# Interleaving the high and low halves of the activations, so that a stationary block is read with a stride of 8 bytes

## The chip, the cores and the metric

The kernel runs on one core of a Trainium2 chip. The metric is the device time of one execution in microseconds; the median of the runs shown counts. Five engines work side by side in a core: TensorE (PE; its weight loads have a row of their own, PEld), VectorE (DVE), ScalarE (ACT), GpSimd (POOL) and SyncE (SP), which issues most of the DMAs here.

## The reference

A decoder trunk of two layers on 256 tokens of width 2048, in float32. Layer 0 mixes tokens by retention (8 heads), layer 1 by sliding-window attention (32 heads of 64, 4 key/value heads, window 128). After the mixer each layer has a SwiGLU block of width 5632 and a gated per-layer embedding; one norm ends it. Cut to what matters:

```python
for i in range(DEPTH):
    h = rmsnorm(x, norm_mix[i])
    x = x + (retention_mixer(h, ...) if i % 2 == 0 else swa_mixer(h, ...))
    x = x + swiglu(rmsnorm(x, norm_ffn[i]), ffn_w_in[i], ffn_w_out[i])
    gate = jax.nn.sigmoid(rmsnorm(x, norm_ple[i]) @ ple_w_gate[i])
    x = x + gate * (p[i] @ ple_w_proj[i])
return rmsnorm(x, norm_final)
```

Nearly all of its arithmetic is matmuls of 256 tokens with large weight matrices: two matrices in every mixer, two in every SwiGLU block, two in every embedding step.

## The kernel before, in words

**Products in three parts.** A float32 product is made of three matmuls in TensorE's faster 32-bit type (float32r). Each operand is split into `hi`, the value rounded to that type, and `lo`, what is left over; the product is `x_hi * w_hi + x_hi * w_lo + x_lo * w_hi`. `split` (lines 209 to 217) makes both halves: ScalarE writes `hi` (line 211, or 214 with a scale), then VectorE computes `lo` from the source and `hi` (line 212, or 215).

**What is stationary and what moves.** The activations, turned so that features lie on the partitions, are the stationary operand: a block is 128 features by 128 tokens, so 128 float32 in each partition. The weights move: 512 columns, which is 2048 bytes in each partition. `multiply` (line 143) issues for each unit of 256 rows of a weight matrix two blocks of features, two blocks of tokens and the three products of lines 161, 162 and 163: twelve matmuls, each with a weight load of its own.

```python
xh, xl = u.lhs.hi[:, k, sl], u.lhs.lo[:, k, sl]
nc.tensor.matmul(ch.acc[n], xh, hi[:, j, cols], start=first, stop=False)
nc.tensor.matmul(ch.acc[n], xh, lo[:, j, cols], start=False, stop=False)
nc.tensor.matmul(ch.acc[n], xl, hi[:, j, cols], start=False, stop=last)
```

**The stationary tiles.** `Lhs` (line 44) holds a pair of tiles of one layout, [128 partitions, blocks of features, 256 tokens]. There are five pairs: `xTh`/`xTl` (line 107; 16 blocks; the normed input of every input projection, gate and up matrix), `pTh`/`pTl` (line 108; 2 blocks; the per-layer embedding), `yTh`/`yTl` (line 308; 32 blocks; retention's output), `oTh`/`oTl` (line 409; 16 blocks; attention's output) and `hTh`/`hTl` (line 579; 44 blocks; the SwiGLU block's hidden layer). The first two lie in a pool that lasts, the others in a pool of their stage, opened when the stage's first unit is due. Every stationary tile of these, and every tile of the moving weights, begins at an address that leaves 160 when divided by 256 bytes; a pad of 56 floats ahead of the stage pools (line 106) is part of what makes it so.

**The order of the work.** `run` goes through the units of all stages in one sequence. For each it issues the DMA of the unit five places ahead, splits the weights of the unit three places ahead, issues the matmuls, and then lets every waiting generator in `side` take one step. Those generators do what follows a finished block of results: 32x32 transposes on VectorE (line 236), then splits into the stationary tiles (`place`, line 277, and lines 388, 552, 586, 619). TensorE meets a few other matmuls on the way: retention's scores (lines 329, 331) and outputs (356 to 358, whose stationary tiles are pairs of their own that `Lhs` does not hold), attention's scores (460), its probability transposes (512) and its outputs (544). In the last stage the final gate block is cut into pieces of 512, 256 and 256 columns.

Of the kernel before, what the change touches and what calls it, by code (L numbers as in the profile page):

```python
# [11 lines left out]
F32 = mybir.dt.float32  # L12
F32R = mybir.dt.float32r
# [5 lines left out]
P = 128  # L19
D = 2048  # L20
S = 256
# [3 lines left out]
KD = D // P  # L25
# [3 lines left out]
RET_OUT_K = RH * RV // P  # L29
# [3 lines left out]
FF_K = FF // P  # L33
PLE = 256
PLE_K = PLE // P
# [8 lines left out]
class Lhs:  # L44


    def __init__(self, tiles=None):
        self.tiles = tiles
        self.ready = set()

    hi = property(lambda self: self.tiles[0])
    lo = property(lambda self: self.tiles[1])


class Chunk:
# [32 lines left out]
def tile_trunk(ctx, tc, ins, out):  # L88
    nc = tc.nc
    pool = ctx.enter_context(tc.tile_pool(name="persist", bufs=1))  # L90
# [13 lines left out]
    turned = ctx.enter_context(tc.tile_pool(name="turned", bufs=1))  # L104

    turned.tile([P, 56], F32, name="pad")
    xT = [pool.tile([P, KD, S], F32R, name=n) for n in ("xTh", "xTl")]
    pT = [pool.tile([P, PLE_K, S], F32R, name=n) for n in ("pTh", "pTl")]


    side = deque()
# [97 lines left out]
    def split(hi, lo, src, scale=None):  # L209
        if scale is None:  # L210
            nc.scalar.activation(hi, src, AF.Copy)  # L211
            nc.vector.tensor_tensor(lo, src, hi.bitcast(F32), op=ALU.subtract)  # L212
        else:
            nc.scalar.activation(hi, src, AF.Copy, scale=scale)  # L214
            nc.vector.scalar_tensor_tensor(  # L215
                out=lo, in0=src, scalar=scale, in1=hi.bitcast(F32), op0=ALU.mult, op1=ALU.subtract
            )
# [9 lines left out]
    def transposes(dst, src):  # L227

        n = P // SQ
        src = src.rearrange("p t (k c f) -> p t k c f", c=n, f=SQ)  # L230
        dst = dst.rearrange("p k (t c f) -> p t k c f", c=n, f=SQ)
        for i in range(n * n):
            if i % STEP == 0:
                yield
            a, b = divmod(i, n)
            nc.vector.transpose(  # L236
                dst[b * SQ : (b + 1) * SQ, :, :, a, :], src[a * SQ : (a + 1) * SQ, :, :, b, :]
            )
# [5 lines left out]
    class Norm:  # L244
# [3 lines left out]
        def __init__(self, which, layer):  # L248
            self.gain = None if which is None else gains[:, which, layer, :]
            self.ss = self.inv = None  # L250
            self.lhs = Lhs(xT)
            self.seen = 0
# [28 lines left out]
    def residual(stage, norm, c, late=0):  # L281

        def done(acc):
            for t in range(NT):
                xc = xs[:, t, c * NW : (c + 1) * NW]
                nc.vector.tensor_tensor(xc, xc, acc[t], op=ALU.add)  # L288
            norm.chunk(c)

            def later():
                for _ in range(late):
                    yield
                xt = turned.tile([P, 4, S], F32, name="xt")
                yield from transposes(xt, xs[:, :, c * NW : (c + 1) * NW])
                yield from norm.places(c, xt)

            return later()

        return done  # L300


    def retention(norm, next_norm, w_in, w_out):
        yl = Lhs()

        def opened(st, pools):
            st.pool = pools.enter_context(tc.tile_pool(name="ret", bufs=2, reuse_waits="tile"))
            yl.tiles = [st.pool.tile([P, RET_OUT_K, S], F32R, name=n, bufs=1) for n in ("yTh", "yTl")]

        stage = Stage(opened)  # L310

        def head(h):
# [90 lines left out]
    def swa(norm, next_norm, w_in, w_out):  # L403
        ol = Lhs()
        st = {}

        def opened(stage, pools):
            sp = stage.pool = pools.enter_context(tc.tile_pool(name="swa", bufs=1, reuse_waits="tile"))
            ol.tiles = [sp.tile([P, KD, S], F32R, name=n) for n in ("oTh", "oTl")]
            st["rel"] = rel = sp.tile([P, 3 * P], F32, name="rel")  # L410
            nc.sync.dma_start(rel, ins["rel"])
            st["sink"] = sink = sp.tile([P, SH], F32, name="sink")
            nc.sync.dma_start(sink, ins["sinks"].to_broadcast([P, SH]))

        stage = Stage(opened)

        def kv_done(acc):
# [145 lines left out]
        n = KD // KU  # L563
# [10 lines left out]
    def ffn(layer, norm, next_norm):  # L574
        hl = Lhs()

        def opened(stage, pools):
            fp = stage.pool = pools.enter_context(tc.tile_pool(name="ffn", bufs=1, reuse_waits="tile"))
            hl.tiles = [fp.tile([P, FF_K, S], F32R, name=n) for n in ("hTh", "hTl")]
            pt = turned.tile([P, 4, S], F32, name="xt")[:, 0:PLE_K, :]  # L580
            nc.sync.dma_start(pt, ins["pT"][layer])

            def later():
                for _ in range(3):
                    yield
                split(*pT, pt)

            side.append(later())

        stage = Stage(opened)  # L590

        def pair(j):
            st = []

            def gate_done(acc):
                h = stage.pool.tile([P, NT, NW], F32, name="h")
                for t in range(NT):
                    nc.scalar.activation(h[:, t, :], acc[t], AF.Silu, scale=norm.inv[:, t : t + 1])
                st.append(h)

            def up_done(acc):
                h = st[0]
                for t in range(NT):
                    nc.vector.scalar_tensor_tensor(
                        out=h[:, t, :],
                        in0=acc[t],
                        scalar=norm.inv[:, t : t + 1],
                        in1=h[:, t, :],
                        op0=ALU.mult,
                        op1=ALU.mult,  # L610
                    )

                def later():
                    hT = turned.tile([P, 4, S], F32, name="xt")
                    yield from transposes(hT, h)
                    for i in range(0, 4, 2):
                        yield
                        ks = slice(4 * j + i, 4 * j + i + 2)
                        split(hl.hi[:, ks, :], hl.lo[:, ks, :], hT[:, i : i + 2, :])
                        hl.ready.update(range(ks.start, ks.stop))  # L620

                return later()

            stage.linear(ins["ffn_w_in"][layer], j, norm.lhs, gate_done)
            stage.linear(ins["ffn_w_in"][layer], FF // NW + j, norm.lhs, up_done)

        for j in range(FF // NW):
            pair(j)
        for c in range(4):
            stage.linear(ins["ffn_w_out"][layer], c, hl, residual(stage, next_norm, c))  # L630
        return stage
# [235 lines left out]
```

## Time and profile before

| | |
|---|---|
| median of the runs | 2625.12 us (2624.99 to 2625.26) |
| the profiled execution, its own time | 2625.55 us |
| its span, first to last instruction | 2623.4 us |
| granted TensorE clock, mean | 0.998 of full |
| weight loads and matmuls | 11643 each |
| DMA | 497.79 MB, mean 190 GB/s |

How to read it: the profile lists one execution. A line of a group names the source line, the engine, the operation, what it writes and reads, the size, the count, the busy time and the mean time of one; behind the second bar stands the idle time of the engine ahead of these instructions, and what ended it. Matmuls are pipelined and their ends are modelled, so the duration of one is longer than the step from one start to the next. A weight load (PEld) runs while the matmul ahead of it streams.

### The profile page before, as it was taken

How to read it: one execution, taken by the hardware profiler on the slowest of the kernel's cores; microseconds unless marked ns; L12 is line 12 of the kernel's file. 1: busy time of each engine (PE TensorE's matmuls, PEld its weight loads, DVE VectorE, ACT ScalarE, POOL GpSimd, SP SyncE). 2: the span in 40 equal slices, each digit the busy share in tenths (PEclk: the TensorE clock that was granted, in tenths of full speed). 3: DMA queues.
4: the chain of work that ended last, by engine and by line, in shares of the span. 5: the costliest groups of instructions: out<-in, count | busy, mean ns of one | idle time of the engine just before them, and what ended most of it. 6: DMA issues, size and time to landing. Idle time of an engine off the chain costs nothing.

```text
span 2623.4 us, 31295 instructions
## 1 busy us (share of the span) xinstructions
PE 2609.3 (99%) x11643; PEld 2145.1 (82%) x11643; DVE 1814.6 (69%) x2563; ACT 1223.1 (47%) x1531; POOL 15.1 (1%) x31
## 2 busy tenths in 40 slices
PE   9999999999999999999999999999999999999998
PEld 7888888888888888888888887777888888888887
DVE  7777777766676767676555886887757575755565
ACT  6444444444444444444444555555444444444444
POOL 0000000000000000000000000000000000000000
PEclk9999999999999999999999999999999999999999
DMA  8555555566666666666666665446666666666664
GB/s 288 187 187 187 186 186 180 182 192 186 203 191 195 191 196 189 199 187 200 193 193 194 191 196 163 126 145 188 189 198 191 197 191 198 189 197 194 193 209 144
DMA packets 139481, 497.79 MB, mean 190 GB/s; under 512 B 15808, under 2 KB 16960, under 8 KB 139200
## 3 DMA queue, kind: packets, MB, share of 16 engines
q1 hardware_dynamic: 139040, 495.73, 60.1%
q8 instruction: 91, 1.49, 0.3%
q14 instruction: 62, 0.51, 0.1%
q10 hardware_dynamic: 288, 0.07, 0.0%
HBM read 493.63 MB, written 2.10 MB: 189 GB/s over the span
## 4 chain that ended last, share of the span: by engine, by line
PE 95%; DVE 3%; issue 1%; DMA 1%; ACT 0%; ACTq 0%; POOLq 0%; POOL 0%; SPq 0%; DVEq 0%
PE acc L163 31%; PE acc L161 31%; PE acc L162 31%; DVE xt L236 1%; DVE lo L212 1%; PE at L460 1%; PE tr L512 0%; PE at L544 0%; DMA raw<-in_ret_w_in 0%; PE at L329 0%; DVE xTl L215 0%; PE at L358 0%; PE at L356 0%; PE at L357 0%; DVE xs L288 0%
## 5 line engine op out<-in xcount | busy, mean ns | idle before, releaser
L212 DVE TENSOR_TENSOR lo<-raw,hi 128x1024 fp32r<-128x1024 f32 (+1 forms) x929 | 1131.4, 1221 | 700.5 <-ACT hi L211 693.1
L211 ACT ACTIVATE hi<-raw 128x1024 fp32r<-128x1024 f32 (+1 forms) x929 | 980.7, 1058 | 1185.9 <-PE acc L163 1075.2
L161 PE MATMUL acc<-hi,xTh 128*128 128x512 f32 x2592 | 1010.8, 390 | 1.8 <-ACT xTh L214 1.7
L162 PE MATMUL acc<-lo,xTh 128*128 128x512 f32 x2592 | 1009.1, 389 | 1.4 <-DVE lo L212 1.4
L163 PE MATMUL acc<-hi,xTl 128*128 128x512 f32 x2592 | 1009.0, 389 | 0.7 <-DVE xTl L215 0.7
L161 PEld LDWEIGHTS acc<-hi,xTh 128*128 128x128 f32 x2592 | 487.4, 188 | 105.5 <-issue 2.9
L162 PEld LDWEIGHTS acc<-lo,xTh 128*128 128x128 f32 x2592 | 487.3, 188 | 103.7 <-DVE lo L212 3.1
L163 PEld LDWEIGHTS acc<-hi,xTl 128*128 128x128 f32 x2592 | 487.2, 188 | 102.4 <-DVE xTl L215 1.5
L161 PE MATMUL acc<-hi,hTh 128*128 128x512 f32 x704 | 274.1, 389 | 0.0
L162 PE MATMUL acc<-lo,hTh 128*128 128x512 f32 x704 | 274.1, 389 | 0.0
L163 PE MATMUL acc<-hi,hTl 128*128 128x512 f32 x704 | 274.1, 389 | 0.0
L236 DVE STREAM_TRANSPOSE xt<-h 32x256 f32<-32x256 f32 x352 | 153.4, 436 | 6.8
L163 PEld LDWEIGHTS acc<-hi,hTl 128*128 128x128 f32 x704 | 132.2, 188 | 27.5
L162 PEld LDWEIGHTS acc<-lo,hTh 128*128 128x128 f32 x704 | 132.2, 188 | 27.3
L161 PEld LDWEIGHTS acc<-hi,hTh 128*128 128x128 f32 x704 | 132.2, 188 | 27.3
L236 DVE STREAM_TRANSPOSE xt<-xs 32x256 f32<-32x256 f32 x320 | 139.5, 436 | 6.0
L162 PE MATMUL acc<-lo,yTh 128*128 128x512 f32 x256 | 99.7, 389 | 0.0
L161 PE MATMUL acc<-hi,yTh 128*128 128x512 f32 x256 | 99.7, 389 | 0.0
L163 PE MATMUL acc<-hi,yTl 128*128 128x512 f32 x256 | 99.7, 389 | 0.0
L214 ACT ACTIVATE xTh<-xt,gains 128x256 fp32r<-128x256 f32 x80 | 35.7, 499 | 64.5 <-DVE xt L236 60.0
L236 DVE STREAM_TRANSPOSE xt<-qk 32x256 f32<-32x256 f32 x128 | 55.8, 436 | 9.8 <-ACT qk L321 7.8
L236 DVE STREAM_TRANSPOSE xt<-y 32x256 f32<-32x256 f32 x128 | 55.9, 436 | 2.5
(128 smaller groups left out, 1170.8 us busy)
## 6 DMA issues: line engine op xcount, KB each, us to landing
raw<-in_ffn_w_in SPq DMA_DIRECT2D x352, 512.0 KB, 4.2
raw<-in_ret_w_in SPq DMA_DIRECT2D x191, 512.0 KB, 3.6
raw<-in_ffn_w_out SPq DMA_DIRECT2D x176, 512.0 KB, 4.0
raw<-in_ret_w_out SPq DMA_DIRECT2D x64, 512.0 KB, 3.7
raw<-in_ple_w_gate SPq DMA_DIRECT2D x64, 512.0 KB, 4.2
raw<-in_swa_w_in SPq DMA_DIRECT2D x40, 512.0 KB, 3.7
raw<-in_swa_w_out SPq DMA_DIRECT2D x32, 512.0 KB, 3.6
raw<-in_ple_w_proj SPq DMA_DIRECT2D x8, 512.0 KB, 3.8
```

The source lines that it names most:

```text
L161: nc.tensor.matmul(ch.acc[n], xh, hi[:, j, cols], start=first, stop=False)
L162: nc.tensor.matmul(ch.acc[n], xh, lo[:, j, cols], start=False, stop=False)
L163: nc.tensor.matmul(ch.acc[n], xl, hi[:, j, cols], start=False, stop=last)
L211: nc.scalar.activation(hi, src, AF.Copy)
L212: nc.vector.tensor_tensor(lo, src, hi.bitcast(F32), op=ALU.subtract)
L214: nc.scalar.activation(hi, src, AF.Copy, scale=scale)
L236: nc.vector.transpose(dst[b * SQ : (b + 1) * SQ, :, :, a, :], src[a * SQ : (a + 1) * SQ, :, :, b, :])
L460: nc.tensor.matmul(ats[e][:, 0:P] if b == 0 else ats[e][:, P : 3 * P], qT[sl, i, b * P : (b + 1) * P], kT[sl, j, 0 : (b + 1) * P], start=True,
```

## The change

Each pair of tiles becomes one tile with a last axis of 2: element `[..., 0]` is `hi`, `[..., 1]` is `lo`. The views `hi` and `lo` thus have a stride of 8 bytes along the tokens, for ScalarE and VectorE that write them and for TensorE that loads a block of them. A block of 128 tokens spans 1024 bytes. The moving weights keep their layout, and so do the stationary tiles of lines 356 to 358. Three pads are added ahead of the stages' tiles: 16 floats (64 bytes) for `yT`, 48 floats (192 bytes) for `oT`, 32 floats (128 bytes) for `hT`; `xT` and `pT` begin where `xTh` and `pTh` began. The four kinds of tiles so begin 0, 64, 128 and 192 bytes, modulo 256, behind the place of the moving weights.

```diff
 class Lhs:
-    def __init__(self, tiles=None):
-        self.tiles = tiles
+    def __init__(self, tile=None):
         self.ready = set()
-
-    hi = property(lambda self: self.tiles[0])
-    lo = property(lambda self: self.tiles[1])
+        if tile is not None:
+            self.take(tile)
+
+    @staticmethod
+    def shape(blocks):
+        return [P, blocks, S, 2]
+
+    def take(self, tile):
+        self.hi, self.lo = tile[:, :, :, 0], tile[:, :, :, 1]
...
-    xT = [pool.tile([P, KD, S], F32R, name=n) for n in ("xTh", "xTl")]
-    pT = [pool.tile([P, PLE_K, S], F32R, name=n) for n in ("pTh", "pTl")]
+    xT = pool.tile(Lhs.shape(KD), F32R, name="xT")
+    pT = pool.tile(Lhs.shape(PLE_K), F32R, name="pT")
...
-            yl.tiles = [st.pool.tile([P, RET_OUT_K, S], F32R, name=n, bufs=1) for n in ("yTh", "yTl")]
+            st.pool.tile([P, 16], F32, name="pad", bufs=1)
+            yl.take(st.pool.tile(Lhs.shape(RET_OUT_K), F32R, name="yT", bufs=1))
...
-            ol.tiles = [sp.tile([P, KD, S], F32R, name=n) for n in ("oTh", "oTl")]
+            sp.tile([P, 48], F32, name="pad")
+            ol.take(sp.tile(Lhs.shape(KD), F32R, name="oT"))
...
-            hl.tiles = [fp.tile([P, FF_K, S], F32R, name=n) for n in ("hTh", "hTl")]
+            fp.tile([P, 32], F32, name="pad")
+            hl.take(fp.tile(Lhs.shape(FF_K), F32R, name="hT"))
...
-                split(*pT, pt)
+                q = Lhs(pT)
+                split(q.hi, q.lo, pt)
```

## The prediction, made before the result was known

> **What bounds the kernel now.** I read the page first: the span, the engines' busy time, and the chain that ended last.
>
> ```profile
> span 2623.4 us, 31295 instructions
> ...
> PE 2609.3 (99%) x11643; PEld 2145.1 (82%) x11643; DVE 1814.6 (69%) x2563; ACT 1223.1 (47%) x1531; POOL 15.1 (1%) x31
> ...
> PE 95%; DVE 3%; issue 1%; DMA 1%; ACT 0%; ACTq 0%; POOLq 0%; POOL 0%; SPq 0%; DVEq 0%
> ```
>
> TensorE is never free: 2609.3 of 2623.4 us, and 95% of the chain. So the time is the number of matmuls times the step from one matmul to the next, and every other engine matters only where it makes PE wait. Second, the groups of matmuls by form, for their numbers (columns: count, then busy us and mean ns of one; the ns include a matmul's run-out, which overlaps the next, so they are not the step).
>
> ```profile
> L161 PE MATMUL acc<-hi,xTh 128*128 128x512 f32 x2576 | 1006.3, 391 | 1.8 <-ACT xTh L214 1.7
> L161 PE MATMUL acc<-hi,hTh 128*128 128x512 f32 x704 | 274.1, 389 | 0.0
> L161 PE MATMUL acc<-hi,yTh 128*128 128x512 f32 x256 | 99.7, 389 | 0.0
> L161 PE MATMUL acc<-hi,oTh 128*128 128x512 f32 x128 | 50.7, 397 | 0.0
> L161 PE MATMUL acc<-hi,pTh 128*128 128x512 f32 x32 | 12.5, 389 | 0.0
> L161 PE MATMUL at<-hi,xTh 128*128 128x256 f32 x16 | 4.5, 283 | 0.0
> L161 PE MATMUL acc<-hi,xTh 128*128 128x256 f32 x16 | 4.5, 280 | 0.0
> ```
>
> Lines 162 and 163 issue one matmul for each of line 161, so the matmuls whose stationary operand the change touches are 3 x (2576 + 704 + 256 + 128 + 32 + 16 + 16) = 3 x 3728 = **11184 of 11643**: xT 7824, hT 2112, yT 768, oT 384, pT 96.
>
> Third, the step, from a window of nothing but such matmuls (columns: window, its length, then busy us and count of PE, of PEld, and on).
>
> ```profile
> 900.00:1300.00 400.00, 400.00 (x1767) 331.32 (x1766) 264.17 (x330) 175.75 (x185) 0.00 (x0) 1.00 0.62 194
> ```
>
> 400 us / 1767 = **226.4 ns**, at granted clock 1.00. 11184 x 226.4 ns = 2532 us, 97% of the span: one ns on the step is 11.2 us, 0.43%. About 2% (52 us) is what a measurement of this kernel can tell from no change; that is a step 4.7 ns longer or shorter.
>
> Fourth, is the step as short as it can be? The last stage has runs of matmuls with 256 columns (six of them, then three with 512):
>
> ```profile
> 2594.05 0.28 PE L161 MATMUL acc<-hi,xTh 128*128 128x256 f32 x1
> ...
> 2594.76 0.40 PE L161 MATMUL acc<-hi,xTh 128*128 128x512 f32 x1
> ...
> 2595.46 0.28 PE L161 MATMUL acc<-hi,xTh 128*128 128x256 f32 x1
> ```
>
> Six steps in 0.71 us: 118.3 ns with 256 columns. From 256 to the usual 512 columns the step grows by 226.4 - 118.3 = 108 ns, so streaming 512 columns takes 2 x 108 = 216 ns (an estimate from these rows), and **10.5 ns of a step are something else**: 11184 x 10.5 ns = 117 us, 4.5% of the time. The change can win no more than about that through the matmuls.
>
> Fifth, what the 10.5 ns hang on. After an interruption by other matmuls the same three instructions step otherwise:
>
> ```profile
> 47.30 0.40 PE L163 MATMUL acc<-hi,xTl 128*128 128x512 f32 x1
> 47.53 0.40 PE L161 MATMUL acc<-hi,xTh 128*128 128x512 f32 x1
> 47.77 0.40 PE L162 MATMUL acc<-lo,xTh 128*128 128x512 f32 x1
> 48.00 0.39 PE L163 MATMUL acc<-hi,xTl 128*128 128x512 f32 x1
> ...
> 50.06 0.39 PE L163 MATMUL acc<-hi,xTl 128*128 128x512 f32 x1
> ```
>
> 47.30 to 48.00 is three steps of 233 ns; 47.30 to 50.06 is twelve of 230 ns; then the step settles at 226.4. Operands and shapes are the same, only the timing of the weight load against the running matmul differs. So at least part of the extra is not a fixed price: something in the load and the running stream gets in each other's way. That is what a different stride of the load can touch, in either direction.
>
> **The change part by part.** *It removes and adds no instruction*: each `hi`/`lo` pair of tiles becomes one tile with the same bytes, and three pads of 64, 192 and 128 bytes move the tiles behind them. DMAs, semaphores' causes and the order of issue stay; no step is moved past a queue.
>
> *The weight loads.* 11184 loads now read 128 elements 8 bytes apart, over 1024 bytes of a partition instead of 512. The rows of loads:
>
> ```profile
> L161 PEld LDWEIGHTS acc<-hi,hTh 128*128 128x128 f32 x704 | 132.2, 188 | 27.3
> L163 PEld LDWEIGHTS acc<-hi,yTl 128*128 128x128 f32 x256 | 48.1, 188 | 10.0
> L544 PEld LDWEIGHTS at<-pT,vs 128*64 128x64 f32 x48 | 3.7, 136 | 5.5 <-issue 4.5 <-DVE lo L212 0.7 <-DVE sc L470 0.4
> ```
>
> Busy plus idle per load is (132.2 + 27.3) / 704 = 226.6 ns, the step again. 64 columns fewer take 188 - 136 = 52 ns less, so 128 columns are read in 104 ns, the rest is latency. Even read at half speed (208 ns) the load fits under the step, and a load that is late by its latency alone costs nothing, since the 256-column run steps at 118 ns with loads that last 188. The cover is the matmul itself; past 216 ns of reading it would be gone, and each further ns would cost 11.2 us. No row of this trace has a strided load, so the step is bounded from both sides: at best the 10.5 ns vanish (-117 us), at worst the 10.5 ns double (+117 us); with the mean of the 10.5 and of the 233 - 216 = 17 ns that an unsettled stream shows, about 14 ns each, +157 us. I take **0**, because all rows nearest to it (128 columns, 4 bytes each, hT, yT, xT alike) show one step whichever tile is read, and because the number of elements stays: a load that is fed element by element gets in the stream's way as often as before.
>
> The rule that weighs against 0: the Trainium skill, "SBUF — State Buffer", section "Specifications (TRN2)", says that SBUF is organized in 16-byte lines, needs at least two hits per line for full bandwidth, and that each crossing to a new line costs. At 8 bytes a line still gets two hits, so by the first half the load keeps its speed; by the second half it crosses 64 lines instead of 32. No run here shows a line's price; by "crossings count", the sum would be that of the slower rival below, by "two hits suffice" it is 0. The skill's "TensorE: Matmul & The Clock Gate", section "Step-by-step: what each phase is for", says further that the load and the moving operand have independent read ports, so that a load takes no bandwidth from a running matmul; by it the stride changes nothing, while the 233 ns steps above show that the two are not quite independent in this kernel.
>
> *The splits.* ScalarE now writes `hi`, and VectorE reads `hi` and writes `lo`, at 8-byte steps.
>
> ```profile
> L214 ACT ACTIVATE xTh<-xt,gains 128x256 fp32r<-128x256 f32 x80 | 35.7, 499 | 64.5 <-DVE xt L236 60.0 <-PE acc L162 4.3
> L215 DVE SCALAR_TENSOR_TENSOR xTl<-xt,gains,xTh 128x256 fp32r<-128x256 f32 x80 | 34.3, 479 | 5.2 <-ACT xTh L214 5.2
> L211 ACT ACTIVATE hTh<-xt 128x512 fp32r<-128x512 f32 x44 | 25.4, 626 | 25.8 <-DVE xt L236 25.8
> L212 DVE TENSOR_TENSOR hTl<-xt,hTh 128x512 fp32r<-128x512 f32 x44 | 28.3, 685 | 0.0
> ```
>
> They total some 61 us on ACT and 63 on DVE here (and less than half as much again for yT, oT, pT and the first x blocks). If a strided write took twice as long, both engines would still have room (ACT is busy 47%, DVE 69%), and PE hides it. What PE waits for now:
>
> ```profile
> PE acc L161 <- ACT xTh L214: 1.7, 1, 1.7
> PE acc L162 <- DVE lo L212: 1.4, 4, 0.5
> PE at L745 <- POOL sq L742: 1.3, 1, 1.3
> PE acc L163 <- DVE xTl L215: 0.7, 2, 0.4
> ```
>
> 5.1 us in all, 2.4 of it for split activations. Without the cover, the last block of each of five stage changes would be late: 5 x 4 splits x 0.48 us = 10 us at most. Nothing suggests that they get faster. I take 0, with 0 to +10 for the range.
>
> *One tile instead of two.* If the program orders by tile, the first matmul on a block (`hi` alone) may also have to wait for the `lo` of that block: one DVE split, 0.48 us, at the few places where a block is split just in time. That lies in the same 10 us.
>
> **Sum.** The profiled execution took 2625.6 us (span 2623.4, and 2.2 around it); the median of the runs shown is 2625.1, half a us less. 2625.6 + 0 (loads) + 0 (splits) = **2625.6 us**. Its own range: the mean disturbed step of 230 ns is 3.5 ns over the settled one, 39 us; taken on both sides, with the 10 us of the splits above: 2587 to 2675.
>
> **The rivals.**
>
> *Slower: the load is fetched in units wider than 4 bytes.* Place: the read side of TensorE, under every one of the 11184 matmuls. If what gets in the way is a fetch of 8 bytes or more, interleaving doubles the fetches for 128 elements, and the 10.5 ns become 21: step 237, 2625.6 + 117 = **2743 us**; with 14 ns, 2783. It decides from the first matmul on and needs only that fetches, not elements, collide. For it: the extra does depend on the load. Against it: nothing in the trace shows a unit.
>
> *Faster: the two streams stop crossing.* The moving operand goes through 512 x 4 = 2048 bytes in 216 ns, 9.5 bytes per ns; the load through 512 bytes in 104 ns, 4.9; interleaved, 1024 in 104, 9.8. Now the moving stream overtakes the load; with the change both run side by side at nearly one speed, and if the extra comes from meeting at the same place of a memory that repeats every so many bytes, it could go: 2625.6 - 117 = **2508 us**. For it: the tile sizes put every stationary and moving tile of the kernel before at the same remainder modulo 256 bytes (160), and the pads spread yT, hT and oT to 64, 128 and 192 bytes from that. Against it: a load that is about as fast already exists, that of the transposes, and the step beside it is no shorter:
>
> ```profile
> L224 PEld LDWEIGHTS tr<-ident,q 128*128 128x128 f32 x32 | 3.7, 140 | 0.6
> ```
>
> and, in order of time (start, us):
>
> ```profile
> 1572.48 0.39 PE L163 MATMUL acc<-hi,xTl 128*128 128x512 f32 x1
> 1572.71 0.60 PE L224 MATMUL tr<-ident,kd 128*128 128x128 f32 x4
> ```
>
> Its reading lasts 140 - (188 - 104) = 56 ns, 512 bytes at 9.1 per ns, and the matmul above it takes 230 ns.
>
> *The offset decides, tile by tile.* Then the change does its work for some tiles only. One ns is 7.8 us on xT, 2.1 on hT, 0.8 on yT, 0.4 on oT. If xT loses 10.5 ns and the others gain them, or the reverse, 82 - 35 = 47 us either way: 2579 or **2672 us**, within 2%.
>
> **How the numbers follow.** The chances: no change of step 0.36; slower by fetches 0.34; faster by side-by-side streams 0.25; mixed by offset 0.05. The first is ahead by little: the evidence that load and stream disturb each other takes from it, the equal steps of all tiles give to it. Slower stands before faster because more fetches is the plainer result of a stride, and the quick load of the transposes brings no gain. Faster by over 2%: 0.25; within 2%: 0.36 + 0.05 = 0.41; slower by over 2%: 0.34. Cases of both signs hold more than half, so the range must reach both: down to 2495, a little below the full gain, and up to 2785, the slower case with 14 ns; beyond lies about one chance in ten. The likeliest case alone is 2587 to 2675.
>
> **What would show it.** Right: a window of pure matmuls again holds about 442 per 100 us (1767 in 400), for xT, hT, yT and oT alike, loads near 188 ns, and PE's waits for ACT and DVE under 15 us. Slower rival: about 422 per 100 us, with the span grown evenly over all stages. Faster rival: about 463 per 100 us. Mixed: the stretches of FFN output (hT) and retention output (yT) differ from those reading xT. A load that lasts some 104 ns longer would show reading at half speed. The splits are wrong if the groups of lines 211 to 215 into these tiles grow and PE waits for them by more than 10 us. The prediction fails if the settled step moves by more than 4.7 ns.

## The result, and the profile after

The change makes the kernel slower: 2689.89 us (2689.58 to 2690.20) against 2625.12 us, a ratio of 1.0246 with a 95% interval of 1.0229 to 1.0262. The profiled execution's span is 2688.0 us, 64.6 us more than before. The page of the changed kernel, the lines that answer to those of before:

```profile
span 2688.0 us, 31295 instructions
...
PE 2674.4 (99%) x11643; PEld 2212.6 (82%) x11643; DVE 1815.9 (68%) x2563; ACT 1226.8 (46%) x1531; POOL 15.1 (1%) x31
...
PE 99%; DVE 0%; DMA 0%; issue 0%; ACT 0%; SPq 0%; ACTq 0%; POOLq 0%; POOL 0%
```

The number of instructions is the same, PE is as full as before, and the whole 65 us are in PE's busy time. The window of pure matmuls (PE's busy us and count first) holds 1718 of them instead of 1767:

```profile
900.00:1300.00 400.00, 400.00 (x1718) 331.90 (x1717) 250.38 (x305) 170.83 (x176) 0.00 (x0) 1.00 0.61 189
```

400 us / 1718 = 232.8 ns, where it was 226.4. (A window also counts the matmuls that reach over its edges, and from 1244 us on this one reads hT.) The groups of weight loads tell it tile by tile. Busy time plus the idle time behind the second bar, divided by the count, is the step. The groups of xT before, then those of after:

```profile
L161 PEld LDWEIGHTS acc<-hi,xTh 128*128 128x128 f32 x2592 | 487.4, 188 | 105.5 <-issue 2.9 <-ACT xTh L214 2.2 <-ACT hi L211 0.9
L162 PEld LDWEIGHTS acc<-lo,xTh 128*128 128x128 f32 x2592 | 487.3, 188 | 103.7 <-DVE lo L212 3.1 <-issue 0.7
L163 PEld LDWEIGHTS acc<-hi,xTl 128*128 128x128 f32 x2592 | 487.2, 188 | 102.4 <-DVE xTl L215 1.5 <-issue 0.7
```

```profile
L167 PEld LDWEIGHTS acc<-hi,xT 128*128 128x128 f32 x2592 | 501.6, 194 | 109.2 <-issue 3.0 <-ACT hi L217 2.2 <-ACT xT L220 1.8
L168 PEld LDWEIGHTS acc<-lo,xT 128*128 128x128 f32 x2592 | 501.4, 193 | 104.2 <-DVE lo L218 0.9 <-issue 0.7
L169 PEld LDWEIGHTS acc<-hi,xT 128*128 128x128 f32 x2592 | 501.2, 193 | 105.0 <-DVE xT L221 0.8 <-issue 0.7
L167 PEld LDWEIGHTS acc<-hi,hT 128*128 128x128 f32 x704 | 137.8, 196 | 25.2
...
L169 PEld LDWEIGHTS acc<-hi,yT 128*128 128x128 f32 x256 | 49.7, 194 | 9.2
...
L167 PEld LDWEIGHTS acc<-hi,oT 128*128 128x128 f32 x128 | 24.9, 195 | 6.8 <-issue 2.3
```

Summed over the three lines of code and compared with the same groups of before (where the three groups of xT came to 1773.5 us): xT 1822.6, that is 49.1 us more; hT 10.2 more (231.5 ns a step instead of 226.6), yT 2.6 (230.1 instead of 226.7), oT 1.6, pT 0.8. Together 64.3 us, of a difference of the spans of 64.6. By the start times in the trace, settled xT matmuls lie 233.3 ns apart, where it was 226.7; hT goes round a pattern of seven steps (229, 233, 230, 228, 232, 232, 236 ns), yT one of four (229, 229, 229, 233). Seven steps fit neither the three products nor the twelve matmuls after which the code repeats.

The weight load itself grew only from 188 to 193 to 196 ns. PE's waits for other engines, by the view of waits, are no longer than before (3.5 us without the line of the warm-up matmuls, `at L755` here; 3.8 before):

```profile
PE acc L167 <- ACT xT L220: 1.3, 1, 1.3
PE acc L167 <- ACT hi L217: 1.3, 1, 1.3
PE at L755 <- POOL sq L752: 1.3, 1, 1.3
PE acc L168 <- DVE lo L218: 0.5, 1, 0.5
PE acc L169 <- DVE xT L221: 0.4, 1, 0.4
```

Writing with the stride costs ScalarE a little and VectorE nothing: 499 to 518 ns and 626 to 670 ns on ACT, 479 to 480 and 685 to 687 on DVE. PE hides it. The rows of ACT, then of DVE:

```profile
L220 ACT ACTIVATE xT<-xt,gains 128x256 fp32r<-128x256 f32 x80 | 36.7, 518 | 56.7 <-DVE xt L242 54.5 <-PE acc L168 2.1
...
L217 ACT ACTIVATE hT<-xt 128x512 fp32r<-128x512 f32 x44 | 27.2, 670 | 17.2 <-DVE xt L242 17.2
```

```profile
L221 DVE SCALAR_TENSOR_TENSOR xT<-xt,gains,xT 128x256 fp32r<-128x256 f32 x80 | 34.3, 480 | 5.3 <-ACT xT L220 5.3
...
L218 DVE TENSOR_TENSOR hT<-xt,hT 128x512 fp32r<-128x512 f32 x44 | 28.3, 687 | 0.0
```

So the question is only why a step takes 230 to 233 ns now, and 226.7 before.

### The profile page after: what moved, and what is told of

It is laid out like the page before. It is cut to its first block, busy times and chain, and to the rows that moved or that the text cites. A ratio compares the mean times of both kernels' runs of the same rounds, so it can differ in the third digit from the quotient of the medians.

```text
span 2688.0 us, 31295 instructions
## 1 busy us (share of the span) xinstructions
PE 2674.4 (99%) x11643; PEld 2212.6 (82%) x11643; DVE 1815.9 (68%) x2563; ACT 1226.8 (46%) x1531; POOL 15.1 (1%) x31
## 4 chain that ended last, share of the span: by engine, by line
PE 99%; DVE 0%; DMA 0%; issue 0%; ACT 0%; SPq 0%; ACTq 0%; POOLq 0%; POOL 0%
PE acc L167 32%; PE acc L169 32%; PE acc L168 32%; PE at L468 1%; PE tr L520 0%; PE at L552 0%; DMA raw<-in_ret_w_in 0%; PE at L336 0%; PE at L365 0%; PE at L363 0%; PE at L364 0%; DVE lo L218 0%; PE tr L230 0%; PE at L338 0%; ACT hi L217 0%
## 5 line engine op out<-in xcount | busy, mean ns | idle before, releaser
L167 PE MATMUL acc<-hi,xT 128*128 128x512 f32 x2592 | 1023.3, 395 | 2.7 <-ACT xT L220 1.3
L169 PE MATMUL acc<-hi,xT 128*128 128x512 f32 x2592 | 1021.0, 394 | 0.4 <-DVE xT L221 0.4
L168 PE MATMUL acc<-lo,xT 128*128 128x512 f32 x2592 | 1020.8, 394 | 0.5 <-DVE lo L218 0.5
L167 PEld LDWEIGHTS acc<-hi,xT 128*128 128x128 f32 x2592 | 501.6, 194 | 109.2 <-issue 3.0
L169 PEld LDWEIGHTS acc<-hi,xT 128*128 128x128 f32 x2592 | 501.2, 193 | 105.0 <-DVE xT L221 0.8
L168 PEld LDWEIGHTS acc<-lo,xT 128*128 128x128 f32 x2592 | 501.4, 193 | 104.2 <-DVE lo L218 0.9
L168 PE MATMUL acc<-lo,hT 128*128 128x512 f32 x704 | 276.9, 393 | 0.0
L167 PE MATMUL acc<-hi,hT 128*128 128x512 f32 x704 | 276.9, 393 | 0.0
L169 PE MATMUL acc<-hi,hT 128*128 128x512 f32 x704 | 276.9, 393 | 0.0
L167 PEld LDWEIGHTS acc<-hi,hT 128*128 128x128 f32 x704 | 137.8, 196 | 25.2
L169 PEld LDWEIGHTS acc<-hi,hT 128*128 128x128 f32 x704 | 137.8, 196 | 25.2
L168 PEld LDWEIGHTS acc<-lo,hT 128*128 128x128 f32 x704 | 137.7, 196 | 25.2
L167 PE MATMUL acc<-hi,yT 128*128 128x512 f32 x256 | 100.4, 392 | 0.0
L168 PE MATMUL acc<-lo,yT 128*128 128x512 f32 x256 | 100.4, 392 | 0.0
L169 PE MATMUL acc<-hi,yT 128*128 128x512 f32 x256 | 100.4, 392 | 0.0
```

## The experiments

Two theories stood at the start. "More fetches": a load with a stride of 8 bytes goes through twice as many pieces of memory, and each gets in the way of the running matmul. "The streams cross", with its sharper form "the offset decides": what counts is where the load's addresses lie against those of the moving weights.

**The change without its pads.**

```diff
-            st.pool.tile([P, 16], F32, name="pad", bufs=1)
-            sp.tile([P, 48], F32, name="pad")
-            fp.tile([P, 32], F32, name="pad")
```

> The change without its three pads: every stationary tile begins at the same place modulo 256 bytes as the moving weights. Theory 'more fetches' (the stride alone sets the step): the steps of yT, hT and oT stay where the changed kernel has them (230, 231.4 and some 234 ns), time 2690 within 3 us. Rival 'the offset decides': yT, hT and oT take the step of xT, whose offset was 0 already (233.3 ns), so 768 x 3.3 + 2112 x 1.9 ns = 6.5 us more, some 2696 us.

Measured: 2696.65 us, ratio 1.0272 (1.0256 to 1.0287), against 1.0246 for the change; the two were timed in different sessions, but the trace agrees: hT and yT take the step of xT.

```profile
L167 PEld LDWEIGHTS acc<-hi,hT 128*128 128x128 f32 x704 | 136.2, 193 | 28.1
...
L167 PEld LDWEIGHTS acc<-hi,yT 128*128 128x128 f32 x256 | 49.5, 193 | 10.1
```

(136.2 + 28.1) / 704 = 233.4 ns, and 232.8 ns for yT. The time is what the rival gave, and the offset counts at a stride of 8. The run also shows what interleaving does where nothing else moves: at the offset of before it costs 71.7 us, against 2624.9 us of the kernel before beside it. The pads of the change gave back 6.8 of these.

**The pads alone.** The kernel before, two separate tiles, with the same three pads ahead of `yTh`, `oTh` and `hTh`.

```diff
+            st.pool.tile([P, 16], F32, name="pad", bufs=1)
             yl.tiles = [st.pool.tile([P, RET_OUT_K, S], F32R, name=n, bufs=1) for n in ("yTh", "yTl")]
...
+            sp.tile([P, 48], F32, name="pad")
             ol.tiles = [sp.tile([P, KD, S], F32R, name=n) for n in ("oTh", "oTl")]
...
+            fp.tile([P, 32], F32, name="pad")
             hl.tiles = [fp.tile([P, FF_K, S], F32R, name=n) for n in ("hTh", "hTl")]
```

> The kernel before (two separate tiles, stride 4 bytes) with the three pads of 64, 192 and 128 bytes. Theory 'the stride alone': every step stays at 226.7 ns, time 2625 within 3 us. Rival 'the offset decides': yT, hT and oT leave 226.7 ns while xT stays; at the 3 ns that separate the tiles in the changed kernel this is up to 3264 x 3 ns = 10 us, of either sign.

Measured: 2643.86 us, ratio 1.0071 (1.0056 to 1.0086). Not one stride was changed.

```profile
L161 PEld LDWEIGHTS acc<-hi,xTh 128*128 128x128 f32 x2592 | 487.4, 188 | 107.0 <-issue 2.9 <-ACT hi L211 2.2 <-ACT xTh L214 2.2
...
L161 PEld LDWEIGHTS acc<-hi,hTh 128*128 128x128 f32 x704 | 132.8, 189 | 30.7
...
L161 PEld LDWEIGHTS acc<-hi,yTh 128*128 128x128 f32 x256 | 48.2, 188 | 11.5
```

xT stays; hT steps at 232.2 ns and yT at 233.2, up from 226.6 and 226.7 before, and slower than the same offsets interleaved (231.5 and 230.1). Over the three lines of code hT costs 12.1 us more than before and yT 5.0, of a difference of the spans of 18.3. That the stride alone sets the step falls here: the offset acts at a stride of 4 just as well, and by more than was expected.

**A stride of 16 bytes.** The halves of two feature blocks lie side by side; no pads.

```diff
-        return [P, blocks, S, 2]
+        return [P, blocks // 2, S, 4]
...
+    def at(self, half, k, sl=slice(0, S)):
+        return self.tile[:, k // 2, sl, 2 * (k % 2) + half]
...
-                xh, xl = u.lhs.hi[:, k, sl], u.lhs.lo[:, k, sl]
+                xh, xl = u.lhs.at(0, k, sl), u.lhs.at(1, k, sl)
```

> Halves of two feature blocks side by side, so that a stationary block has a stride of 16 bytes over 2048 bytes; no pads. Theory 'more fetches': going from 4 to 8 bytes doubled the 16-byte pieces of a block (32 to 64) and cost 6.9 ns on xT, so doubling again (128) costs 13.8 ns more, step 247 ns, time 2696 + 154 = 2850 us, the load itself visibly longer. Rival 'the streams cross' (what counts is how fast the load's addresses run against the moving ones: half as fast at 4 bytes, level at 8, twice as fast at 16): the step lies within the 226 to 239 ns seen so far, time 2625 to 2750 us. A load that is read at half speed shows as some 104 ns more per load.

Measured: 2732.55 us, ratio 1.041 (1.0393 to 1.0427).

```profile
L175 PEld LDWEIGHTS acc<-hi,xT 128*128 128x128 f32 x2592 | 802.8, 310 | 1.1 <-DVE xT L227 1.1
...
L175 PEld LDWEIGHTS acc<-hi,hT 128*128 128x128 f32 x704 | 217.9, 310 | 0.0
```

The window of 900 to 1300 us:

```profile
900.00:1300.00 400.00, 400.00 (x1704) 400.00 (x1704) 261.66 (x314) 177.39 (x177) 0.00 (x0) 1.00 0.60 187
```

A load takes 310 ns instead of 193, and PEld is busy for the whole window; yet the settled step is 235.0 ns by the starts (400 us / 1704 = 234.7) and not 247. The 2850 us of "more fetches" are missed by 117 us, and the time lies in the range of the rival (2625 to 2750). What sets the step here is not separated: with 256 moving columns, in the next run, loads of this stride follow each other every 233.3 ns, so their own pace may be what 235.0 ns shows, and not the offset.

**Only matmuls.** Five kernels leave the computation out. They run, for each case, the kernel's pattern of products 16 times (96 matmuls) on two fixed moving tiles, every case of float32r at least twice, in both orders; a number below is the mean distance of the starts, read from the trace, after the first two dozen or so. Each of the five kernels ran once, at a mean granted clock of 0.995 to 0.999.

```python
for i in range(n_sets):
    for b in range(2):
        nc.tensor.matmul(acc[b][:, :n], hi[b], mov[0][:, :n], start=i == 0, stop=False)
        nc.tensor.matmul(acc[b][:, :n], hi[b], mov[1][:, :n], start=False, stop=False)
        nc.tensor.matmul(acc[b][:, :n], lo[b], mov[0][:, :n], start=False, stop=i == n_sets - 1)
```

The first goes through strides and a few offsets:

```diff
+    [(f"s1o{4 * o}", 1, o, NW) for o in (0, 4, 8, 16, 32, 48)]
+    + [(f"s2o{4 * o}", 2, o, NW) for o in (0, 1, 2, 4, 8, 16, 32, 48)]
...
+    + [(f"s4o{4 * o}", 4, o, NW) for o in (0, 1, 16, 32, 48)]
+    + [(f"s8o{4 * o}", 8, o, NW) for o in (0, 16)]
```

> The computation is left out; only matmuls of one stationary tile per case with the same two moving tiles, 96 in a row, for strides of 4, 8, 12, 16 and 32 bytes, offsets of 0 to 192 bytes modulo 256 from the moving tiles, and 256 or 512 columns; each case twice, in both orders. Theory 'more fetches': the step rises with the stride up to 16 bytes (226.7, 233, 237 to 240, 247 ns), stays there at 32, and does not care about the offset; with 256 columns the same extra. Rival 'the streams cross': at a stride of 8 bytes the step depends on the offset by 5 ns or more, at 4 bytes it does not, and the strides are not in order.

Measured, 512 columns: stride 4: 226.7 ns at offset 0, but 233.3 at 32 and 64, 232.3 and 233.3 at 128, 228.9 at 192, and at 16 226.7 in one pass and 233.3 in the other, where only the order of the cases differed. Stride 8: 230.0 to 233.4. Stride 12: 233.3 and 235.6. Stride 16: 235.0 to 240.0. Stride 32: 244.4. With 256 columns strides 4 and 8 both take 120.0 ns, and 16 takes 233.3. So the whole-kernel steps of before and after are there without the rest of the kernel: at a stride of 8 the offsets 0, 64 and 128 give 233.3, 230.0 and 231.4 ns, as xT, yT and hT have them in the changed kernel, and a stride of 16 at offset 0 gives 235.0. At a stride of 4 the offset moves the step as far as the change did. Neither theory holds as it was put: against "more fetches", the offset counts, 32 bytes are slower than 16, and with 256 columns 8 bytes cost no more than 4; against "the streams cross", the offset counts at a stride of 4, and at 8 by 3.4 ns and not by 5.

The loads (mean ns before the last bar), for 512 columns at strides of 12 and 32 bytes, and for 256 at 16 and at 8:

```profile
L58 PEld LDWEIGHTS a<-mlo,s3o 128*128 128x128 f32 x128 | 32.4, 253 | 0.0
...
L58 PEld LDWEIGHTS a<-mlo,s8o 128*128 128x128 f32 x192 | 63.2, 329 | 0.0
...
L58 PEld LDWEIGHTS a<-mlo,s4n 128*128 128x128 f32 x64 | 21.1, 329 | 0.0
...
L58 PEld LDWEIGHTS a<-mlo,s2n 128*128 128x128 f32 x64 | 12.5, 195 | 0.0
```

**One offset for all tiles.** The short runs gave numbers to forecast whole kernels by: 230.0 ns at a stride of 8 and offset 64, 233.3 at a stride of 4 and offset 64. Both kernels put every stationary tile, xT too, 64 bytes behind the moving weights; the first interleaved, the second with separate tiles. The pad after `pT` shifts the weights, the others the stages' tiles. The edit shown is that of the interleaved kernel against the change; the separate one gets the same three pads and one of 16 floats ahead of `yTh`.

```diff
     pT = pool.tile(Lhs.shape(PLE_K), F32R, name="pT")
+    pool.tile([P, 48], F32, name="pad")
...
-            sp.tile([P, 48], F32, name="pad")
+            sp.tile([P, 16], F32, name="pad")
...
-            fp.tile([P, 32], F32, name="pad")
+            fp.tile([P, 16], F32, name="pad")
```

> Interleaved as in the change, but every stationary tile, xT and pT too, begins 64 bytes behind the moving weights modulo 256. Theory 'the offset decides, at either stride': all steps go to the 230.0 ns that the matmuls alone showed at a stride of 8 and offset 64; against 2696.65 us at offset 0, 11184 x 3.3 ns = 37 us less, some 2660 us. Rival 'the stride alone': the time stays at 2690 to 2697 us.

> Two separate tiles as before the change (stride 4 bytes), every stationary tile 64 bytes behind the moving weights. Theory 'the offset decides, at either stride': all steps go to the 233.3 ns that the matmuls alone showed at a stride of 4 and offset 64; 2625 + 11184 x 6.65 ns = 2625 + 74, some 2699 us, which would be slower than the same offset interleaved. Rival 'the stride alone': near 2625 us. In between (some 2645) would mean that the steps settle in another pattern in the whole kernel than in the short runs.

Measured: interleaved 2661.76 us, ratio 1.014 (1.0123 to 1.0157); separate 2693.57 us, ratio 1.0263 (1.0248 to 1.0279). Both come as the short runs said, to 2 and 5 us. The order is turned round: at this offset the interleaved tiles are 32 us faster than the separate ones. Their hT groups, interleaved first:

```profile
L168 PEld LDWEIGHTS acc<-hi,hT 128*128 128x128 f32 x704 | 136.8, 194 | 25.2
```

```profile
L162 PEld LDWEIGHTS acc<-hi,hTh 128*128 128x128 f32 x704 | 131.6, 187 | 32.5
```

230.1 and 233.1 ns. The separate tiles with the shorter load (187 ns) have the longer step.

**All offsets.**

```diff
+    [(f"off{o}by4x", 1, o // 4, NW) for o in range(0, 256, 8)]
+    + [(f"off{o}by8x", 2, o // 4, NW) for o in range(0, 256, 16)]
```

> The computation is left out; only matmuls, 96 in a row per case: 32 offsets of 8 bytes at a stride of 4, 16 offsets of 16 bytes at a stride of 8, each twice, and 96 matmuls with bfloat16 operands. Theory 'the addresses of load and stream meet': at a stride of 4 the step takes several values between 226.7 and 236 ns, and offset 0 is at or near the lowest; at a stride of 8 between 229 and 235, none as low as 226.7. Rival: some offset reaches 220 ns or less, then a better kernel than before exists. bfloat16 (half the bytes on both sides): 216 ns if the extra is the reading of 4-byte elements, 226.7 if every change of the stationary block costs it.

Measured: stride 4, 32 offsets: 226.7 to 234.3 ns, mean 231.9; 226.7 at 0 and 120 in both passes, at 40 and 216 in one of two, 228.3 at 240, most others 230 to 233.3. Stride 8, 16 offsets: 230.0 to 233.4, mean 232.4. Both are as the theory had them. bfloat16, one pass, with one moving tile and the two token blocks in turn: 215.8. The rows at offset 0 of both strides, at 120, and of bfloat16:

```profile
L54 PEld LDWEIGHTS a<-mlo,off0by4x 128*128 128x128 f32 x80 | 15.5, 193 | 3.2
...
L54 PEld LDWEIGHTS a<-mlo,off0by8x 128*128 128x128 f32 x64 | 12.4, 193 | 2.6
...
L54 PEld LDWEIGHTS a<-mlo,off120by4x 128*128 128x128 f32 x64 | 12.0, 188 | 2.5
...
L67 PEld LDWEIGHTS <-bsta 128*128 128x128 bf16 x96 | 10.0, 105 | 29.0 <-ACT bsta L60 15.8 <-issue 3.8
```

(off0by4x came first and its row holds the cold start.) On the mean over offsets the stride costs 0.5 ns, 6 us of the 64 that the change lost. The kernel before stood on one of the few good offsets, and no offset tried is better than it.

**Other mixtures, and the halves apart.** Stride 4 with only the lo weights, only the second block of tokens, or only the lo half moved; and a stride of 8 with hi and lo in different places.

```diff
+    [(f"wlo{o}x", o // 4, 0, 0) for o in range(0, 256, 8)]
+    + [(f"block{o}x", 0, o // 4, 0) for o in range(16, 256, 16)]
+    + [(f"half{o}x", 0, 0, o // 4) for o in range(16, 256, 16)]
...
+    for name, shift in (("apartx", 0), ("apart64x", 16)):
```

> The computation is left out; only matmuls, 96 in a row per case, each case twice. Stride of 4 with everything at offset 0 except one: the lo weights (31 offsets of 8 bytes), the second block of tokens (15 offsets of 16 bytes), or the lo half of the activations (15). Then a stride of 8 bytes with hi and lo far apart, at offsets 0 and 64. Theory 'the addresses of load and stream meet': with any one of the addresses moved the step leaves 226.7 for values between 227 and 234 ns, and none goes under 226; with the halves apart the step is what it is with the halves side by side (233.3 at offset 0, 230 to 233.3 at 64), because it is the stride that counts and not the neighbour. Rival: some mixture gives a pattern of 220 to 225 ns, and a better kernel than before exists; or the halves apart go back to 226.7, and it is the sharing of a place by hi and lo that costs.

Measured: of 61 mixtures none is under 226.7 ns; block and half at 16, 144 and 240 reach it (in one pass of two at 16, and half at 144), the others lie between 228.9 and 236.7. The theory misses there in part: some mixtures stay at 226.7, and a few go above its 234. The halves apart: 233.3 at offset 0, 230.0 at 64, as side by side. So it is not the sharing of a tile, and among all that was tried at 512 columns there is no step shorter than that of the kernel before.

**What the load reads.**

```diff
+    ("same16x", P, 0, 1, NW),
+    ("cols96x", 96, 1, 1, NW),
+    ("cols64x", 64, 1, 1, NW),
+    ("cols32x", 32, 1, 1, NW),
+    ("move8x", P, 1, 2, NW),
...
+    ("n384x", P, 1, 1, 384),
...
+    ("n384by8x", P, 2, 1, 384),
```

> The computation is left out; only matmuls, 96 in a row per case, each case twice, all at offset 0: the stationary block with 128, 96, 64 and 32 columns, with one element read 128 times (stride 0), the moving operand with a stride of 8 bytes, both with 8, and 384 and 448 columns. Theory 'the extra is the load reading beside the stream': it shrinks with the columns loaded (226.7 ns at 128, about 221 at 64, about 219 at 32, towards the 216 of bfloat16), and 384 columns cost as much extra as 512. Theory 'places of a memory meet': with stride 0 the load stays at one place and the extra goes to 0 to 3 ns. Rival 'a fixed price of changing a 4-byte block': 226.7 ns in all of these. A moving operand of stride 8: slower than 226.7 by either of the first two, since the stream then crosses twice as many places.

Measured: 226.7 ns with 128 columns; 230.0 with 96, 230.0 with 64, 231.7 with 32; 231.1 with one element read 128 times; 173.3 with 384 columns at either stride; 206.7 and 202.7 in the two passes with 448; 451 to 453 with the moving operand at a stride of 8.

```profile
L65 PEld LDWEIGHTS a<-mhi,move8x 128*128 128x128 f32 x64 | 13.3, 208 | 15.7 <-issue 15.7
...
L65 PEld LDWEIGHTS a<-mhi,n384by8x 128*128 128x128 f32 x64 | 12.4, 194 | 0.0
...
L65 PEld LDWEIGHTS a<-mhi,same16x 128*128 128x128 f32 x64 | 12.0, 188 | 3.0
...
L65 PEld LDWEIGHTS a<-mhi,cols32x 128*32 128x32 f32 x64 | 7.0, 109 | 7.9
```

This fells my theory of what lies under the offset. A load of a quarter of the columns, over in 109 ns, leaves a longer step; and a load that stays at one place does not make the extra vanish, as the theory had asked. The three predictions on record for the narrower loads and for the single element all miss. That the strided moving operand is slower came true.

**Numbers of columns.** What was left was a beat that the handover from one matmul to the next might wait for.

```diff
+    (f"n{n}by{4 * s}x", P, s, 1, n)
+    for s in (1, 2)
+    for n in (512, 510, 508, 504, 500, 496, 492, 488, 480, 472, 464, 456, 448, 432, 416, 400, 384, 320)
```

> The computation is left out; only matmuls, 96 in a row per case, each case twice, all at offset 0, with 320 to 512 moving columns, at strides of 4 and 8 bytes. What the run before left: the extra does not follow the elements that the load reads. Theory 'the handover waits for a beat of 6.67 ns': the steps stand on stairs of 6.67 ns (173.3, 206.7, 213.3, 220, 226.7, 233.3) and not on a straight line, and stride 8 takes the next stair at some numbers of columns and not at others (equal at 384, one stair up at 512). Rival 'a straight line': step = columns x 0.4167 ns + 13.3 at a stride of 4 and + 20 at a stride of 8 for every number of columns, within 1 ns.

Measured, ns at a stride of 4 and of 8: 512 columns 226.7 and 233.3; 510: 226.7 and 233.3; 508: 227.7 and 226.7; 488: 220.0 both, but 225.9 in one pass at a stride of 4; 480: 216.7 both; 456: 208.9 and 204.5; 432: 195.8 and 193.3; 416: 188.3 and 186.7; 400: 180.0 both; 384: 173.3 both; 320: 146.7 both. From 384 to 512 at a stride of 4 a column costs (226.7 - 173.3) / 128 = 0.417 ns; over that line the extra is never under 13.3 ns, and goes up to 22.6. Neither a straight line nor clean stairs: many steps are multiples of 6.67 ns, others (208.9, 195.8) are means over a longer pattern. And stride 8 is the quicker one at 508, 456, 432 and 416 columns, the slower one at 512, 510, 500, 496 and 464.

```profile
L57 PEld LDWEIGHTS a<-mlo,n456by8x 128*128 128x128 f32 x64 | 12.4, 194 | 0.7
...
L57 PEld LDWEIGHTS a<-mlo,n456by4x 128*128 128x128 f32 x64 | 12.0, 187 | 1.4
```

13.1 us against 13.4 for 64 steps, with the longer load.

## Why the prediction came out as it did

**Right.** PE bounds the kernel, the time is the step times the count, and a ns on the step is 11.2 us: the measured 64.3 us over 11184 matmuls are 5.7 ns. The strided load stays under the step, the splits and the common tile cost PE nothing (waits of 3.5 us). And the settled step is not a fixed price: the 233 ns that the disturbed stream of the trace before had shown for a few matmuls is the step at which xT of the changed kernel settles.

**Wrong: the term "the weight loads", taken as 0.** It should have been 64 us: the settled step of xT moved by 6.6 ns, beyond the 4.7 ns at which the prediction said that it fails. The first reason given was that the nearest rows "all show one step whichever tile is read". They did, but all of those tiles stood at the same offset to the weights, as the rival on the streams itself says ("the same remainder modulo 256 bytes"). Equal steps at one offset say nothing about another offset or another stride. The pads alone show it: hT and yT leave 226.7 ns for 232 to 233 with no stride changed. The second reason, that the number of elements stays, carries nothing either: with a quarter of the elements the step is 231.7 ns. The 10.5 ns of "something else" were a little small too. With 256 columns settled steps take 120.0 ns and not 118.3, which leaves 13.3 ns; in the very rows that gave 118.3, the three matmuls of 512 columns step at 233 ns (2594.76 to 2595.46) and not at 226.4.

**The likeliest case missed, and the range held by its width.** "No change of step" (0.36) was ahead of "slower by fetches" (0.34) and its own range ended at 2675. The measured 2689.89 us lie between it and the slower rival, as the 430 matmuls per 100 us lie between the 442 and the 422 named as signs; that they are inside 2495 to 2785 is luck, since that range was drawn to reach gains and losses alike. Slower by over 2%, which had 0.34, is what came, at half the size that the slower rival gave (2743), and for another reason: fetches do not set the price, since stride 4 with the wrong offset is as slow (2693.57 us at 64) and a quarter of the load is no quicker.

**The faster rival** was wrong in its consequence: equal speed of the two address streams gives no step under 230 ns at 512 columns. It was right that addresses matter. **"The offset decides, tile by tile"** had 0.05 and was nearest to the truth in kind: the steps of the changed kernel differ by tile (233.3, 231.5, 230.1 ns), by the offset. It was wrong in that no tile gained against before.

**Two hits on a line, and crossings.** The prediction weighed two rules of the Trainium skill ("SBUF — State Buffer", "Specifications (TRN2)"): that two hits on a 16-byte line are needed for full bandwidth, and that each crossing to a new line costs. For the load the runs agree with the first: at 8 bytes it grows by 5 to 8 ns, and at 16 bytes, one hit, by 122. For the moving operand they do not: at 8 bytes, two hits, it takes twice as long (453 ns instead of 226.7). That crossings count is not borne out by the step at 8 bytes: twice as many cost 0.5 ns on the mean over offsets.

**What is shown, and what stays open.** Shown: the loss lies in the step alone, and the step follows from the stride together with the offset. At the offset of before the stride costs 71.7 us, on the mean over the offsets, by the short runs, some 6; what the change gave up is a good offset. The pairs of load and matmul settle in a repeating pattern of steps, which depends on the offset, the stride and the columns, and in some cases differed between two passes over the same addresses; the kernel before is in the best pattern found (226.7 ns, 13.3 ns over the columns' own time), and at 512 columns no offset tried at a stride of 8 reaches it. Open: what in the hardware makes these patterns, and why 13.3 ns is the least. Neither the amount that the load reads, nor its way through memory, nor a plain beat explains the runs. That the offset counts modulo 256 bytes was taken from the start and not tested for itself.

## What to carry to other kernels

In a kernel that is one long row of like matmuls, divide a window by its count to get the step, and treat the addresses of stationary and moving tiles against each other as a quantity to be tuned: with float32r operands it was worth 226.7 to 233.3 ns a step, 2.6% of this kernel, without any change to the work. A few dozen matmuls per case in a kernel of their own find such steps; here they forecast two whole kernels to 2 and 5 us. Before a change of layout is costed at nothing because all rows are alike, ask in what the rows are alike: here it was the one thing that the change moved.

## What the runs showed of the hardware that was not expected

- A moving float32r operand with a stride of 8 bytes streams at half speed (451 to 453 ns for 512 columns), while a stationary one with the same stride loads at nearly full speed (193 to 196 ns instead of 188) and falls back from 12 bytes on (253 ns; 310 at 16 bytes, where 256 columns take 233 ns a step instead of 120).
- bfloat16 steps at 215.8 ns for 512 columns; float32r never came nearer than 13.3 ns to its columns' own 0.417 ns each.
- The same instructions at the same addresses can settle at different steps, each for all 96 matmuls of a case: 226.7 or 233.3 ns at offset 16 in the first run of strides, 233.3 or 228.9 at 192 in the run of offsets.
- Writing every second float costs ScalarE 19 ns more for 256 elements and 44 for 512, and VectorE 1 to 2.
